# A decoder step on one core: the third token tile's norm emitted behind all output weights

## The chip, the core and the metric

The kernel runs on one core of a Trainium2 chip. The metric is the device time of one execution in microseconds (us). Before the change it is 3105.05 us, the median of three runs (3102.8 to 3105.16).

## What is computed

One step of a hybrid decoder in float32: a gated convolution layer, then a layer of gated sliding-window attention, for 2048 prompt tokens and 32 sample tokens (model width 1024, 2048 convolution channels). The part around the change is the end of the convolution layer:

```python
c = depthwise_conv(v)                       # 31 taps, 2048 channels
c = silu(layernorm(c) * ln_g + ln_b)        # mean and variance over the channels
y = (c * silu(z)) @ w_out                   # 2048 -> 1024
x = x + y
```

`z` is a third of the layer's input product. The attention layer behind it works on `x`.

## The kernel before, in words

Phase A (line 41) makes the input product in tiles of 128 channels by 416 tokens, gates it, runs the convolution and stores its result `c` and the gate `silu(z)` to tensors in HBM, channels on partitions. Every product is made of three TensorE passes: each operand is split into a rounded half (`hi`) and the rest (`lo`), and hi x hi, hi x lo and lo x hi are summed.

Phase B (line 277) does the norm and the output product in token tiles of 128 tokens: sixteen for the prompt, one of 32 for the samples, which comes second to last. Tile 2 is the third. Per tile it has three steps.

- `norm(pos)` (lines 292 to 323) loads the tile of `c` (L297, 1 MB, into one of three buffers by pos % 3) and the tile of the gate (L303, 1 MB, two buffers by pos % 2). VectorE sums over the channels of a partition (L306), TensorE sums over partitions with a matrix of ones (L308), VectorE subtracts the mean (L309); ScalarE squares in two halves through one PSUM buffer (L312), VectorE sums them (L314), TensorE again (L315); ScalarE takes the root (L317), VectorE the reciprocal (L318) and the product (L319); ScalarE does SiLU with gain and bias in 16 pieces (L321); VectorE multiplies by the gate (L322).
- `split(pos, c)` makes the two halves: a cast on ScalarE (L336, `bmh`) and a subtract on VectorE (L337, `bml`). They have two buffers by pos % 2.
- `out(pos, ...)` runs 48 matmuls for each half of the 1024 output columns (L359 to L361), j = 0 and j = 1, adds `x` (L363), sums squares for the next norm (L368) and stores (L371). `rows(pos)` loads the tile of `x` for it (L344).

The output weights are eight blocks of 512 input rows by 512 columns, four for j = 0 and four for j = 1, each loaded in two DMAs of 512 KB. `Weights.ahead` (L234) loads seven of them into buffers that are used later for other weights; the eighth goes through a staging buffer (L257). `Weights.half` casts each 512 KB on ScalarE (L262, `ho`) and subtracts on VectorE or GpSimd (L265, `lo`).

The order of the work is set in three ways. A planner at build time walks the program with estimated durations and fixes for each engine, and for the queue of DMA issues of SyncE (SP), one order; an instruction that is ready goes first if it was emitted earlier, and `high_priority(offset=n)` counts it as emitted n places earlier. On the chip each engine then works strictly in that order. Third, `issue_after(ins)` ties DMA issues behind another issue of the same queue, with no wait for its landing. `d["pace"]` holds the last such issue: each `norm` sets it to its `c` load, each load of `ahead` ties itself behind it and sets it anew, and the staged pair of L257 ties itself behind it without setting it.

Tiles 0 and 1 are normed while phase A's last products run. Then the weights are emitted: j = 0, then `norm(2)`, then j = 1 (lines 387 to 393), and behind them the loop over the tiles, which norms and splits two tiles ahead of the products.

Of the kernel before, what the change touches and what calls it, by code (L numbers as in the profile page):

```python
# [276 lines left out]
def phase_b(tc, d, kc, tail, outer, then):  # L277
# [6 lines left out]
    with ExitStack() as ctx:  # L284
# [7 lines left out]
        def norm(pos):  # L292
            i = order[pos]
            n = 128 if i < 16 else TS
            t0 = i * 128
            c = (pl if pos % 3 == 2 else pe).tile([128, 16, n], F32, tag=f"c{pos % 3}", name=f"bc{i}")
            d["pace"] = nc.sync.dma_start(c, cs[:, :, t0:t0 + n])  # L297
            sz = pe.tile([128, 16, n], F32, tag=f"sz{pos % 2}", name=f"bsz{i}")
            t = t0
            while t < t0 + n:  # L300
                q, o = divmod(t, CW)
                e = min(t0 + n, (q + 1) * CW)
                nc.sync.dma_start(sz[:, :, t - t0:e - t0], sz_d[q].rearrange("a p t -> p a t")[:, :, o:o + e - t])  # L303
                t = e
            s = pe.tile([128, n], F32, tag=f"s{pos % 2}", name=f"bs{i}")
            nc.vector.tensor_reduce(s, c.rearrange("p a t -> p t a"), axis=AX.X, op=ALU.add)  # L306
            ps = pn.tile([128, 2, 128], F32, tag="st", name=f"bst{i}", bufs=2)
            nc.tensor.matmul(ps[:, 0, :n], lhsT=kc.ones, rhs=s, start=True, stop=True)  # L308
            nc.vector.tensor_tensor(c, c, ps[:, 0, :n].unsqueeze(1).to_broadcast([128, 16, n]), op=ALU.subtract)  # L309
            for h in range(2):  # L310
                sq = pn.tile([128, 8, n], F32, tag="sq", name=f"bsq{i}_{h}")
                nc.scalar.activation(sq, c[:, 8 * h:8 * h + 8], AF.Square)  # L312
                v = pe.tile([128, n], F32, tag=f"v{h}{pos % 2}", name=f"bv{i}_{h}")
                nc.vector.tensor_reduce(v, sq.rearrange("p a t -> p t a"), axis=AX.X, op=ALU.add)  # L314
                nc.tensor.matmul(ps[:, 1, :n], lhsT=kc.ones, rhs=v, start=(h == 0), stop=(h == 1))  # L315
            r = pe.tile([128, n], F32, tag=f"r{pos % 2}", name=f"br{i}")
            nc.scalar.activation(r, ps[:, 1, :n], AF.Sqrt, bias=kc.eps)  # L317
            nc.vector.reciprocal(r, r)  # L318
            nc.vector.tensor_tensor(c, c, r.unsqueeze(1).to_broadcast([128, 16, n]), op=ALU.mult)  # L319
            for a in range(16):  # L320
                nc.scalar.activation(c[:, a], c[:, a], AF.Silu, bias=kc.lnb[:, a:a + 1], scale=kc.lng[:, a:a + 1])  # L321
            nc.vector.tensor_tensor(c, c, sz, op=ALU.mult)  # L322
            return c

        def split(pos, c):
            i = order[pos]
            n = 128 if i < 16 else TS
            at = pl if pos % 2 else pm
            if n == TS:
                m2 = at.tile([128, 16, 2 * n], F32R, tag=f"mh{pos % 2}", name=f"bm{i}")  # L330
                mh, ml = m2[:, :, :n], m2[:, :, n:]
            else:
                m2 = None
                mh = at.tile([128, 16, n], F32R, tag=f"mh{pos % 2}", name=f"bmh{i}")
                ml = at.tile([128, 16, n], F32R, tag=f"ml{pos % 2}", name=f"bml{i}")
            nc.scalar.copy(mh, c)  # L336
            nc.vector.tensor_tensor(ml, c, mh.bitcast(F32), op=ALU.subtract)  # L337
            return mh, ml, m2
# [34 lines left out]
        cc, ms = {}, {}  # L373

        def ahead(c):
            if c < 2:
                cc[c] = norm(c)
                if c == 0:
                    ms[0] = split(0, cc[0])
# [6 lines left out]
        pp = pool("b_o", space=PSUM, side="right")  # L386
        ws = [[], []]
        for j, places in enumerate((("w4h", "w4l", "w5h", "w5l"), ("w6h", "w6l", "xh"))):
            if j:
                cc[2] = norm(2)  # L390
            raws = [wts.ahead(wout[j, h], f"o{j}{h}", tag, wx if tag == "xh" else None) for h, tag in enumerate(places)] + [None]
            for h in range(4):
                ws[j].append(wts.half(wout[j, h], f"o{j}{h}", pool=wx if j * h == 3 else None, raws=raws[h]))
        ms[1] = split(1, cc[1])
        for pos in range(15):
            ms[pos + 2] = split(pos + 2, norm(pos + 2) if pos else cc[2])
            if pos == 14:
                norms.close()
                tr = then(pm)
            m, row = ms.pop(pos), rows(pos)  # L400
            for j in range(2):
                out(pos, m, row, j)
# [601 lines left out]
def program(tc, d):  # L1004
# [15 lines left out]
    with tc.tile_pool(name="dram", bufs=1, space=DRAM) as dp, tc.tile_pool(name="k", bufs=1) as pk:  # L1020
        for k, shape in (("c", [16, 128, TT]), ("x1", [TT, 1024]), ("ss", [TT, 1]), ("xts", [128, 8, 2 * TS]),
                         ("xt0", [16, 128, 2, 8, 128]), ("xt1", [4, 128, 16, 4, 128]), ("xt2", [4, 128, 16, 4, 128]), ("u", [3, T, UW]), ("ks", [3, TS, 512]), ("vs", [3, TS, 512]),
                         ("qs", [3, TS, 512]), ("ns", [256, 6]), ("pn", [256, 6]), ("pv", [2, 8, 128, 512]), ("z", [EARLY, 128, 512])):
            d[k] = dp.tile(shape, F32, name="t_" + k)
        d["sz"] = [dp.tile([16, 128, CW], F32, name=f"t_sz{c}") for c in range(NCH)]
        d["copies"] = copies
        kc = Consts(tc, d, pk)
        tail = phase_a(tc, d, kc)
        with ExitStack() as outer:
            pk2 = outer.enter_context(tc.tile_pool(name="k2", bufs=1, reuse_waits="tile"))  # L1030
            for k, w in (("kvnorm", 8), ("bnorm", 8), ("lng", 16), ("lnb", 16)):
                kc.load(pk2, k, [128, w])
            kc.load(pk2, "knorm", [128, 64], d["knorm"].partition_broadcast(128))
            kc.load(pk2, "qnorm", [128, 64], d["qnorm"].partition_broadcast(128))
            kc.load(pk2, "rope_s", [TS, 24])

            def then(pm):

                pool = lambda name, **k: outer.enter_context(tc.tile_pool(name=name, reuse_waits="tile", **k))
                pk3 = pool("k3", bufs=1)  # L1040
                kc.load(pk3, "mask", [128, 3, 128])
                tr = Trunk(tc, d, kc, pk3, pool("c_f", bufs=2), pm, pool("c_pf", bufs=1, space=PSUM))
                tr.banks = {"pj": ("pj", 2), "tr": ("tr", 1)}
                return tr

            wts, tr = phase_b(tc, d, kc, tail, outer, then)
            tc.keep_in_program_order(nc.scalar.preload_act_table_set("natural_log_exp_and_others"))
            phase_d(tc, d, tr, wts, phase_c(tc, d, tr, wts))
        copies(len(pieces))
# [71 lines left out]
```

## Time and profile before

| | |
|---|---|
| median of three runs | 3105.05 us |
| the profiled execution | 3107.33 us |
| its span on the core | 3105.5 us |
| mean granted clock of TensorE | 0.982 |
| TensorE busy | 2998.1 us, 97% |
| VectorE busy | 2181.9 us, 70% |
| ScalarE busy | 1519.0 us, 49% |
| GpSimd busy | 1281.7 us, 41% |

All times in the text are in us from the start of the span. Phase B lies between about 1095 and 1560. In rows, PE is TensorE, PEld its weight loads, DVE VectorE, ACT ScalarE, POOL GpSimd and SPq the issue queue of SyncE; L297 is line 297 of the kernel, and `bml<-bc,bmh` says that `bml` is written from `bc` and `bmh`. A row of a timeline begins with its start and its length, and may be several instructions of one kind (x2). Idle time of an engine before an instruction stands in brackets at its end, with what ended it. "Granted clock" is the share of 2.4 GHz that TensorE was given; 0.5 is its lower level, 1.2 GHz.

### The profile page before, as it was taken

To read this page: it belongs to the slowest core of one execution; us is meant where nothing else is said; L and a number is where in the kernel's file an instruction comes from. 1 tells how busy PE (TensorE), PEld (TensorE's weight loads), DVE (VectorE), ACT (ScalarE), POOL (GpSimd) and SP (SyncE) were. 2 spreads that over 40 slices of the span, in tenths; PEclk is the share of its full clock that TensorE was granted. 3 is DMA by queue.
4 is the path that set the end of the run, shared out by engine and by line. 5 is a ranking of instruction groups with operands and counts; after the bars stand their busy time and mean duration, and the time that the engine had idled before them with its cause. 6 is when DMAs were issued, how large, how long until landed. Compare 5 with 4: busy or idle time off the path is not lost.

```text
span 3105.5 us, 43118 instructions
## 1 busy us (share of the span) xinstructions
PE 2998.1 (97%) x15994; PEld 2542.9 (82%) x15994; DVE 2181.9 (70%) x3698; ACT 1519.0 (49%) x2913; POOL 1281.7 (41%) x809
## 2 busy tenths in 40 slices
PE   6999999999999989999988999999999989999998
PEld 6999999999999977878766777777777767667786
DVE  6599999999999957667555555666666766345355
ACT  6544555555544445566544444554444634444432
POOL 1799889888877603000013222213333041002342
PEclk9999999999999999999989999999999999999999
DMA  6333333434331266444387666778766565653774
GB/s 196 100 106 100 121 106 128 149 116 129 119 128 64 75 190 201 122 132 119 102 211 184 158 170 159 185 221 213 187 159 156 176 205 175 190 178 116 252 254 160
DMA packets 563404, 482.41 MB, mean 155 GB/s; under 512 B 338321, under 2 KB 474129, under 8 KB 555641
## 3 DMA queue, kind: packets, MB, share of 16 engines
q1 hardware_dynamic: 560601, 475.64, 51.9%
q10 hardware_dynamic: 2592, 4.01, 0.4%
q8 instruction: 126, 2.06, 0.3%
q14 instruction: 85, 0.70, 0.1%
HBM read 345.42 MB, written 221.84 MB: 183 GB/s over the span
## 4 chain that ended last, share of the span: by engine, by line
PE 76%; DMA 9%; DVE 7%; ACT 4%; issue 1%; POOL 1%; SPq 1%; ACTq 0%; POOLq 0%; DVEq 0%
PE pv L68 3%; PE pv L70 3%; PE pv L69 3%; PE pg L68 3%; PE pg L70 3%; PE pg L69 3%; PE pz L70 3%; PE pz L68 3%; PE pz L69 3%; PE s L812 3%; PE pjk L536 3%; PE pjk L539 3%; PE pjk L538 3%; PE pt L831 2%; PE ut L840 2%; PE pjq L538 2%
## 5 line engine op out<-in xcount | busy, mean ns | idle before, releaser
L181 POOL TENSOR_TENSOR ca<-ca,tp 128x1024 f32<-128x1024 f32 x288 | 707.3, 2458 | 175.1 <-ACT tp L180 122.6
L196 DVE SCALAR_TENSOR_TENSOR acc<-vb,cws,acc 128x1024 f32<-128x1024 f32 x608 | 754.6, 1281 | 6.5
L180 ACT ACTIVATE tp<-vb,cws 128x1024 f32<-128x1024 f32 x288 | 329.9, 1151 | 288.7 <-POOL ca L181 280.9
L754 POOL COPY ro<-xt 128x512 f32<-128x512 f32 x128 | 149.4, 1175 | 388.5 <-DMA t_xt<-ro 166.7
L633 POOL TENSOR_TENSOR qb<-qb,kc 128x512 f32<-128x512 f32 x96 | 125.6, 1312 | 321.0 <-DMA qb<-t_qs 247.5
L68 PE MATMUL pv<-xh,wh 128*128 128x416 f32 x640 | 225.1, 352 | 3.1 <-DVE vb L109 2.6
L68 PE MATMUL pg<-xh,wh 128*128 128x416 f32 x640 | 226.2, 354 | 1.6 <-ACT xh L151 1.6
L70 PE MATMUL pg<-xh,wl 128*128 128x416 f32 x640 | 227.2, 355 | 0.0
L70 PE MATMUL pz<-xh,wl 128*128 128x416 f32 x640 | 226.5, 354 | 0.0
L70 PE MATMUL pv<-xh,wl 128*128 128x416 f32 x640 | 226.5, 354 | 0.0
L69 PE MATMUL pg<-xl,wh 128*128 128x416 f32 x640 | 225.2, 352 | 0.1
L68 PE MATMUL pz<-xh,wh 128*128 128x416 f32 x640 | 224.6, 351 | 0.0
L69 PE MATMUL pv<-xl,wh 128*128 128x416 f32 x640 | 224.1, 350 | 0.0
L692 POOL MEMSET spq<- 128x24 f32 x8 | 0.9, 118 | 540.2 <-ACT hq L269 371.2
L69 PE MATMUL pz<-xl,wh 128*128 128x416 f32 x640 | 223.6, 349 | 0.0
L823 ACT ACTIVATE sm<-sm,ngm 128x256 f32<-128x256 f32 (+1 forms) x384 | 172.7, 452 | 95.0 <-DVE ngm L820 92.9
L359 PE MATMUL bpo<-ho,bmh 128*128 128x512 f32 x512 | 205.8, 404 | 11.0 <-ACT ho L262 7.8
L360 PE MATMUL bpo<-lo,bmh 128*128 128x512 f32 x512 | 205.1, 401 | 5.3 <-DVE lo L265 3.1
L361 PE MATMUL bpo<-ho,bml 128*128 128x512 f32 x512 | 203.4, 399 | 2.2 <-DVE bml L337 2.1
L834 ACT COPY qp_p<-pt 128x512 f32<-128x512 f32 x150 | 86.3, 585 | 185.3 <-PE pt L831 184.7
L536 PE MATMUL pjk<-hk,xt 128*128 128x512 f32 x384 | 162.4, 423 | 9.8 <-ACT xt L500 9.6
L536 PE MATMUL pjq<-hq,xt 128*128 128x512 f32 x384 | 156.2, 407 | 4.5 <-ACT hnk L547 4.5
(319 smaller groups left out, 7569.0 us busy)
## 6 DMA issues: line engine op xcount, KB each, us to landing
t_xt<-ro SPq DMA_DIRECT2D x128, 256.0 KB
xt<-t_xt SPq DMA_DIRECT2D x32, 1024.0 KB
wr<-in_win SPq DMA_DIRECT2D x48, 512.0 KB
qb<-t_qs SPq DMA_DIRECT2D x96, 256.0 KB
kc<-in_cache SPq DMA_DIRECT2D x72, 256.0 KB
vc<-in_cache SPq DMA_DIRECT2D x72, 256.0 KB
t_c<-ca SPq DMA_DIRECT2D x16, 1040.0 KB
bc<-t_c SPq DMA_DIRECT2D x16, 1024.0 KB
```

What stands on the lines that cost most here:

```text
L68: nc.tensor.matmul(ps, lhsT=hi[:, k], rhs=xh[:, k], start=(k == 0), stop=False)
L69: nc.tensor.matmul(ps, lhsT=hi[:, k], rhs=xl[:, k], start=False, stop=False)
L70: nc.tensor.matmul(ps, lhsT=lo[:, k], rhs=xh[:, k], start=False, stop=(k == 7))
L180: nc.scalar.activation(tp, src, AF.Copy, scale=cws[:, ct, j:j + 1])
L181: nc.gpsimd.tensor_tensor(dst, dst, tp, op=ALU.add)
L196: nc.vector.scalar_tensor_tensor(out if j == KT - 1 else acc[h], vt[:, h * 1024 + j:h * 1024 + j + 1024], cws[:, ct, j:j + 1], out if j == ...
L359: nc.tensor.matmul(po[:n], lhsT=mh[:, a], rhs=hi, start=(a == 0), stop=False)
L360: nc.tensor.matmul(po[:n], lhsT=mh[:, a], rhs=lo, start=False, stop=False)
L361: nc.tensor.matmul(po[:n], lhsT=ml[:, a], rhs=hi, start=False, stop=(a == 15))
L536: first = nc.tensor.matmul(ps[:n], lhsT=xh[:, j], rhs=hi[:, j], start=(k == 0), stop=False)
L538: nc.tensor.matmul(ps[:n], lhsT=xh[:, j], rhs=lo[:, j], start=False, stop=False)
L823: nc.scalar.activation(sm[:, k], sm[:, k], AF.Exp, bias=ngm[:, h:h + 1], scale=0.125, accum_out=u[:, 520 + h:521 + h])
```

## The change

`norm(2)` is emitted after the weights of both column halves, and not between them. Inside `norm`, for tile 2 alone, the issues of its `c` load and of its gate load are tied behind the issue that `d["pace"]` holds at that moment, which is the last load of `ahead` for j = 1. The loads of `ahead` for j = 1 are then tied behind those of j = 0 and no longer behind tile 2's `c` load. Nothing that is computed changes.

```diff
@@ -294,6 +294,10 @@
             n = 128 if i < 16 else TS
             t0 = i * 128
             c = (pl if pos % 3 == 2 else pe).tile([128, 16, n], F32, tag=f"c{pos % 3}", name=f"bc{i}")
+
+            behind = ExitStack()
+            if pos == 2:
+                behind.enter_context(tc.issue_after(d["pace"].ins))
             d["pace"] = nc.sync.dma_start(c, cs[:, :, t0:t0 + n])
             sz = pe.tile([128, 16, n], F32, tag=f"sz{pos % 2}", name=f"bsz{i}")
             t = t0
@@ -302,6 +306,7 @@
                 e = min(t0 + n, (q + 1) * CW)
                 nc.sync.dma_start(sz[:, :, t - t0:e - t0], sz_d[q].rearrange("a p t -> p a t")[:, :, o:o + e - t])
                 t = e
+            behind.close()
             s = pe.tile([128, n], F32, tag=f"s{pos % 2}", name=f"bs{i}")
             nc.vector.tensor_reduce(s, c.rearrange("p a t -> p t a"), axis=AX.X, op=ALU.add)
             ps = pn.tile([128, 2, 128], F32, tag="st", name=f"bst{i}", bufs=2)
@@ -386,11 +391,10 @@
         pp = pool("b_o", space=PSUM, side="right")
         ws = [[], []]
         for j, places in enumerate((("w4h", "w4l", "w5h", "w5l"), ("w6h", "w6l", "xh"))):
-            if j:
-                cc[2] = norm(2)
             raws = [wts.ahead(wout[j, h], f"o{j}{h}", tag, wx if tag == "xh" else None) for h, tag in enumerate(places)] + [None]
             for h in range(4):
                 ws[j].append(wts.half(wout[j, h], f"o{j}{h}", pool=wx if j * h == 3 else None, raws=raws[h]))
+        cc[2] = norm(2)
         ms[1] = split(1, cc[1])
```

## Rows read from the trace of the kernel before

**Rows 1.** Windows: length, busy us (instructions) by engine, granted clock, DMA share, GB/s
```profile
1210.00:1220.00 10.00, 6.17 (x21) 3.83 (x19) 7.44 (x6) 8.64 (x15) 0.00 (x0) 0.79 0.93 256
1220.00:1230.00 10.00, 9.94 (x32) 8.02 (x33) 6.18 (x5) 2.31 (x2) 0.00 (x0) 0.70 1.04 300
...
1400.00:1540.00 140.00, 140.00 (x630) 112.70 (x629) 87.86 (x67) 86.58 (x164) 0.00 (x0) 1.00 0.37 106
```

**Rows 2.** Waits of TensorE, 1200 to 1230: total us, times, longest
```profile
PE bpo L359 <- ACT bmh L336: 3.0, 2, 2.6
PE bpo L361 <- DVE bml L337: 0.9, 1, 0.9
```

**Rows 3.** Chain of waits in order of time, 1150 to 1240: start, length, what
```profile
1164.03 9.71 DMA bc<-t_c
...
1220.03 7.17 DMA bc<-t_c
```

**Rows 4.** Chain of waits in order of time, 1300 to 1600
```profile
1385.96 2.30 DVE bml L337
```

**Rows 5.** Waits of TensorE, 1230 to 1700
```profile
PE bst L315 <- DVE bv L314: 2.6, 1, 2.6
```

**Rows 6.** Timeline of VectorE, 1150 to 1224
```profile
1152.90 3.65 DVE L306 TENSOR_REDUCE bs<-bc 128x128 f32<-128x2048 f32 x1 [6.63 <-DMA bc<-t_c]
...
1173.76 3.79 DVE L306 TENSOR_REDUCE bs<-bc 128x128 f32<-128x2048 f32 x1 [2.74 <-DMA bc<-t_c]
1178.19 4.49 DVE L309 TENSOR_TENSOR bc<-bc,bst 128x2048 f32<-128x2048 f32 x2 [0.64 <-PE bst L308]
1182.60 1.22 DVE L314 TENSOR_REDUCE bv<-bsq 128x128 f32<-128x1024 f32 x1
...
1186.51 0.68 DVE L363 TENSOR_TENSOR bx<-bpo,bx 128x512 f32<-128x512 f32 x1
...
1192.56 3.79 DVE L306 TENSOR_REDUCE bs<-bc 128x128 f32<-128x2048 f32 x1
1196.26 3.33 DVE L319 TENSOR_TENSOR bc<-bc,br 128x2048 f32<-128x2048 f32 x1
...
1205.93 2.29 DVE L322 TENSOR_TENSOR bc<-bc,bsz 128x2048 f32<-128x2048 f32 x1 [1.96 <-ACT bc L321]
...
1217.72 4.48 DVE L337 TENSOR_TENSOR bml<-bc,bmh 128x2048 fp32r<-128x2048 f32 x2
```

**Rows 7.** Timeline of the queue of SyncE, 1139 to 1181
```profile
1139.79 0.36 SPq L303 DMA_DIRECT2D bsz<-t_sz  x1
1146.30 0.36 SPq L297 DMA_DIRECT2D bc<-t_c  x1
1146.78 13.65 SPq L240 DMA_DIRECT2D rawo<-in_wout  x8
...
1164.03 2.07 SPq L297 DMA_DIRECT2D bc<-t_c  x1
1166.19 4.89 SPq L240 DMA_DIRECT2D rawo<-in_wout  x6
1171.13 2.95 SPq L257 DMA_DIRECT2D rawo<-in_wout  x2
```

**Rows 8.** Timeline of ScalarE, 1174 to 1220
```profile
1175.11 1.05 ACT L262 CAST ho<-rawo 128x1024 fp32r<-128x1024 f32 x1 [8.69 <-DMA rawo<-in_wout]
...
1177.69 1.05 ACT L262 CAST ho<-rawo 128x1024 fp32r<-128x1024 f32 x1 [0.31 <-DMA rawo<-in_wout]
...
1184.32 1.02 ACT L312 ACTIVATE bsq<-bc 128x1024 f32<-128x1024 f32 x1
...
1191.29 0.37 ACT L317 ACTIVATE br<-bst,eps 128x128 f32<-128x128 f32 x1
...
1213.20 3.79 ACT L336 CAST bmh<-bc 128x2048 fp32r<-128x2048 f32 x2
```

## The prediction

> **What bounds the kernel now.** TensorE is the busiest engine, so I looked first for the stretches in which it isn't: the table of windows through the phase that the diff touches. It shows full work nearly everywhere, 140.00 of 140 us from 1400 on, and a hole at 1210 to 1230: 6.17 us of work in the first ten, and a granted clock of 0.79 and 0.70 of 2.4 GHz, so part of it at 1.2 GHz [rows 1]. The waits of TensorE name what made the hole: 3.0 us for the rounded half `bmh` and 0.9 for the rest `bml`, the split of a token tile [rows 2]. By the order of the code the products of tiles 0 and 1 come first; they run with no such wait from 1200 on, so this is the split of tile 2, the tile whose norm the change moves.
>
> Next I read the chain of waits in order of time, to see whether that hole sets the end. It does, though not through TensorE. From 1164.03 the chain is tile 2's load (9.71 us), its norm, its split, then at 1220.03 the load of tile 5 into the buffer that tile 2 has left, and so on, load, norm, split, until a last `bml` at 1385.96 [rows 3, 4]. Behind that TensorE has work without a break. So what counts is the end of tile 2's `bml`, the first L337 of two in a row of 4.48 us: 1217.72 + 2.3 = 1220.0 [rows 6]. Later by x, every later step of that chain is later by x, and so is the end. Earlier by x helps while TensorE has slack to give: 3.0 + 0.9 us of waits, 5.1 us of clock (10 times 0.21 + 10 times 0.30) and a wait of 2.6 us further on, 11.6 us in all [rows 1, 2, 5].
>
> The queue of SP comes third, because the change is about its order. Behind the load at 1146.30 it holds eight weight loads (j = 0), the `c` load at 1164.03, six weight loads (j = 1) and the staged pair of L257 [rows 7]. By the code the six stand behind tile 2's `c`, so 1164.03 is tile 2; 1146.30 is tile 3, whose buffer is tile 0's. Tile 3's first reduce runs at 1152.90, tile 2's at 1173.76, both right on their load [rows 6].
>
> **Part 1, the two loads move.** Tile 2's `c` goes behind the six loads, and, if the planner issues the pair first (it has the higher priority and is free to go), behind all eight. What a weight load costs while the queue is full is read from the casts that wait for it: 1175.11 to 1177.69 is two loads, 1.29 us each [rows 8]. Eight are 10.3 us. The bytes ahead of tile 2's landing are then those that had landed by the end of the pair, so its landing moves from 1173.7 to 1184.0: **+10.3**. Nothing that SP waits for in between gives that back: the gate load `sz` that is taken from 1139.79 frees the head of the queue, but behind it stands tile 3's load, which came 6.5 us later by its own wait [rows 7].
>
> The gate load itself now lands behind `c`. No row shows it in this place; at the weights' rate its 1 MB takes 2.6 us, and the whole issue-to-landing of a `c` of the same size under load was 9.71 [rows 3]. So it lands between 1187 and 1194, and is wanted at 1205.93 by L322 [rows 6]: at least 12 us of cover, cost nothing. Behind it in the queue stand the first two `x` loads and tile 4's `c`. The first `x`, wanted at 1186.51 by L363 [rows 6], then lands 1.29 behind the gate load, between 1188 and 1195. If that add keeps its place on VectorE, just behind tile 2's reduce (1184.0 to 1187.8), it holds the engine, and tile 2's sums behind it, for 0 to 7 us. I take nothing, the end at the weights' rate, and keep the 7 for the upper end of the range.
>
> **Part 2, the six weight loads move up** by what tile 2's `c` took, between 2.6 and 9.7 us. TensorE waits for no weight of j = 1 [rows 2], so this is worth nothing by itself; it is worth something by clearing ScalarE and GpSimd before tile 2 arrives.
>
> **Part 3, what stands between tile 2 and its split.** From landing to the end of `bml` are 1220.0 - 1173.7 = 46.3 us, far more than its own steps. The rest is neighbours on in-order engines, and can be read off [rows 6, 8]:
> - To the square root at 1191.29: 17.5 us from the start of the reduce. Own: 3.8, two matmul groups 0.9, the subtract 2.25, two squares of 1.02 and two sums of 1.22 (one PSUM buffer, so in turn), 11.4. Over: 6.1. The second square starts 0.5 after its buffer is free (1182.60 + 1.22), behind weight casts; I put 0.5 down to handovers; the other 5.1 is tile 3's subtract, squares and sums in between.
> - The reduce of tile 4 in front of L319: 3.8, and L319 itself at 3.33 where such an operation takes 2.29: 1.0, beside a GpSimd weight subtract.
> - L322 ends at 1208.2, `bmh` starts at 1213.20 behind tile 3's SiLUs: 5.0.
> - `bmh` is one of two in 3.79, so it ends at 1215.1, and `bml` starts at 1217.72 behind an add and tile 4's subtract: 2.6.
>
> Without the handovers that is 18.0 us of others: 1.5 of weights (0.5 and L319's 1.0), 10.1 of tile 3, 6.4 of tile 4. In the changed order the weights land before tile 2 does: -1.5. Tile 4's load stays behind tile 2's in the queue, so its 6.4 stays. Tile 3 is the open one: its tile has been there since 1152.9, and with tile 2 10.3 us later it can be through its subtract and squares first, -5.1; or the planner keeps them side by side, 0. Its SiLUs would then also run ahead, up to -5.0. Between these ends I take all of the 5.1 and half of the 5.0, 7.6, because a head start of 10.3 us is about as long as the whole of tile 3's share.
>
> **Sum.** +10.3 - 1.5 - 7.6 = +1.2 us on the end of tile 2's split, and on the end. The profiled execution took 3107.33 us (span 3105.5), 2.3 above the median of 3105.05; on the median that is 3106.2, say 3106. What moves in the TensorE hole itself (its 2.6 us of wait, its clock) isn't added: the chain at 1386 takes it back.
>
> One rule of the Trainium skill speaks against the change: DMA: Bandwidth & Descriptors, section Rules for kernel authors, says to issue a transfer early and wait for it late, so that work covers it. By it a load on the chain that is issued later costs its whole delay, the second rival below; the trace bears out the first half, that this load is on the chain.
>
> **The rivals.**
> *Tile 2 runs alone.* With weights and tile 3 through, and tile 4's reduce and subtract set behind, all 18.0 goes: 10.3 - 18.0 = -7.7, 3097.4. For it: the planner prefers tile 2's steps (emitted first), and tile 4's load too is later. Against: its order is fixed at build time from its own estimates, which in the kernel before put tile 3's SiLUs ahead of tile 2's cast. TensorE's slack of 11.6 us is the floor of this case, 3093; a better interleave for the tiles behind could reach a little further, 3091.
> *The load's delay arrives whole.* VectorE keeps its order, the reduce of tile 2 ahead of tile 3's steps, and stands idle from 1173 on until the tile is there at 1184; tile 3 gains no head start. Then only the 1.5 of weights goes: +8.8, 3113.9. It decides as soon as tile 3 gives back less than 2.6 us, for then the end is over 6.2 us later. For it: VectorE already stands idle for such loads (6.63 and 2.74 us here), and tile 3's subtract ran only beside tile 2's at 1178, 22 us after its reduce was through [rows 6]: its head start was wasted before. Against: nothing of the data forces that. With the 7 us of the `x` load it is 3120.9.
> *It does only part of what it says.* Both loads are tied behind the last of the six, not behind the staged pair. If the planner lets `c` go before the pair, it lands 6 x 1.29 = 7.7 later and not 10.3: -1.4 in all, 3103.7. Against: nothing holds the pair back.
>
> **How the numbers follow.** The forecast has 0.36, with a range of its own from 3099 to 3111; tile 2 alone 0.28; the whole delay 0.28; the partial one 0.08. A measurement of this kernel tells about 0.2%, 6.2 us, from no change. Faster by more: 0.28 and 0.02 of the partial case, 0.30. Slower by more: 0.28. Within: 0.42. The range reaches over both rivals, 3091 to 3120.
>
> **What would show it.** In the changed profile tile 2's reduce should start right on its load near 1184, the fourth and later casts of j = 1 should no longer wait, and `bml` of tile 2 should end near 1221. If VectorE has an idle of some 10 us for a `c` load at 1173 to 1184, the second rival holds; if TensorE runs through 1210 to 1225 without a wait and at the full clock, the first. I would be wrong in the root if the end moves and the end of tile 2's `bml` does not, or if the chain up to 1386 becomes one of TensorE.

## The result and the profile after

The changed kernel is slower. Six runs gave a median of 3119.57 us (3111.02 to 3128.29) beside 3104.58 us (3097.68 to 3109.59) for six of the kernel before: a ratio of 1.0051, 95% interval 1.0034 to 1.0068, or 15.8 us (10.6 to 21.1). A second, later set gave 3116.19 us beside 3099.20 us, 1.0041 (1.0026 to 1.0055), 12.7 us. These ratios are not the quotients of the medians, which lie 15.0 and 17.0 us apart. The profiled execution took 3121.14 us, its span 3119.3 us at a mean granted clock of 0.982, as before. The forecast was 3106.

Lines shift by the added code: L301 is now the `c` load, L307 the gate load, L311 the sum over a partition's channels, L313 and L320 the two products with ones, L314 the mean, L317 the squares, L319 their sums, L322 the root, L324 the product, L326 SiLU, L327 the gate, L341 `bmh`, L342 `bml`, L364 to L366 the output products, L368 the add of `x`. In both profiles `bml` of tile 0 ends at the same time (1146.3 before, 1146.0 after), so times of phase B can be set side by side.

The windows of [rows 1], in the changed kernel (same columns):

```profile
1210.00:1220.00 10.00, 0.00 (x0) 0.00 (x0) 9.62 (x8) 9.61 (x24) 0.00 (x0) 0.54 0.25 86
1220.00:1230.00 10.00, 4.24 (x9) 2.82 (x10) 4.38 (x3) 7.56 (x15) 0.00 (x0) 0.50 0.46 128
1400.00:1540.00 140.00, 140.00 (x630) 113.07 (x629) 92.72 (x69) 89.60 (x172) 0.00 (x0) 1.00 0.38 110
```

The hole in TensorE has become a gap: no product at all from 1210 to 1220, 4.24 us of work in the next ten, at the lower clock, and full work again behind it. Its waits from 1195 to 1235 (total us, times, longest), against 3.0 for `bmh` and 0.9 for `bml` in [rows 2]:

```profile
PE bst L320 <- DVE bv L319: 11.9, 1, 11.9
PE bpo L364 <- ACT bmh L341: 4.8, 1, 4.8
PE bpo L366 <- DVE bml L342: 0.3, 1, 0.3
```

TensorE had run all products of tiles 0 and 1 and stood before tile 4's ones product (the 11.9) and then before tile 2's `bmh`. The chain of waits (start, length, what) has the same links as before [rows 3, 4]: tile 2's cast and subtract, tile 5's load into tile 2's buffer, and so on until it leaves VectorE for good:

```profile
1218.66 5.80 ACT bc L326 x15
1224.46 1.80 ACT bmh L341
1226.28 2.30 DVE bml L342
1228.60 5.98 DMA bc<-t_c
...
1381.93 1.14 DVE bv L319
1383.12 0.49 PE bst L320 x2
```

Tile 2's split ends at 1226.28 + 2.29 = 1228.57: 8.6 us later than before. VectorE's timeline, as in [rows 6], shows where:

```profile
1178.25 3.91 DVE L311 TENSOR_REDUCE bs<-bc 128x128 f32<-128x2048 f32 x1 [5.84 <-DMA bc<-t_c]
1183.44 0.69 DVE L368 TENSOR_TENSOR bx<-bpo,bx 128x512 f32<-128x512 f32 x1 [1.28 <-DMA bx<-in_x]
1191.39 4.49 DVE L314 TENSOR_TENSOR bc<-bc,bst 128x2048 f32<-128x2048 f32 x2 [7.25 <-PE bst L313]
...
1198.66 1.22 DVE L319 TENSOR_REDUCE bv<-bsq 128x128 f32<-128x1024 f32 x1
1199.79 3.80 DVE L311 TENSOR_REDUCE bs<-bc 128x128 f32<-128x2048 f32 x1
...
1203.57 1.22 DVE L319 TENSOR_REDUCE bv<-bsq 128x128 f32<-128x1024 f32 x1
...
1208.55 2.29 DVE L324 TENSOR_TENSOR bc<-bc,br 128x2048 f32<-128x2048 f32 x1
...
1217.17 2.29 DVE L327 TENSOR_TENSOR bc<-bc,bsz 128x2048 f32<-128x2048 f32 x1 [0.34 <-ACT bc L326]
...
1226.28 2.29 DVE L342 TENSOR_TENSOR bml<-bc,bmh 128x2048 fp32r<-128x2048 f32 x1 [5.62 <-ACT bmh L341]
```

Tile 2 is reduced at 1178.25, 4.5 us later than before and not 10.3. But the mean is subtracted only at 1191.39, after 7.25 us in which VectorE stands idle for TensorE. Before, 4.4 us lay between these two starts; now 13.1. The timeline of TensorE says why. First the kernel before, then the changed one:

```profile
1177.70 0.68 PE L308 MATMUL bst<-bs,ones 128*128 128x128 f32 x4 [1.57 <-DVE bs L306]
```

```profile
1190.74 0.39 PE L365 MATMUL bpo<-lo,bmh 128*128 128x512 f32 x1
1190.97 0.38 PE L313 MATMUL bst<-bs,ones 128*128 128x128 f32 x2
...
1192.35 0.38 PE L313 MATMUL bst<-bs,ones 128*128 128x128 f32 x2
...
1204.04 0.38 PE L320 MATMUL bst<-bv,ones 128*128 128x128 f32 x2
```

Before, TensorE stands at the ones products of tiles 2 and 3 (x4) and waits for the reduce. After, tile 2's comes with no wait at all, between output products: the reduce is done at 1182.2, and its turn is 8.8 us later. By the program's order this product stood behind 48 output products and now stands behind 122; tile 3's, also ready since long ago, went with it, to 127. The second ones product has its turn at 1204.04, 4.2 us behind its sum (1198.66 + 1.22). Before, it came at 1190.38, 3.8 us behind its sum (1185.37 + 1.22):

```profile
1190.38 0.38 PE L315 MATMUL bst<-bv,ones 128*128 128x128 f32 x2
```

ScalarE, as in [rows 8], and behind it a row of before that was left out there:

```profile
1204.82 1.03 ACT L317 ACTIVATE bsq<-bc 128x1024 f32<-128x1024 f32 x1 [3.88 <-DVE bv L319]
1205.87 1.28 ACT L322 ACT_TABLE_LOAD   x1
1207.16 0.37 ACT L322 ACTIVATE br<-bst,eps 128x128 f32<-128x128 f32 x1
...
1210.88 6.26 ACT L326 ACTIVATE bc<-bc,k_lnb,k_lng 128x128 f32<-128x128 f32 x16 [0.39 <-DVE bc L324]
...
1218.60 5.86 ACT L326 ACTIVATE bc<-bc,k_lnb,k_lng 128x128 f32<-128x128 f32 x15
1224.37 1.88 ACT L341 CAST bmh<-bc 128x2048 fp32r<-128x2048 f32 x1
```

```profile
1190.00 1.28 ACT L317 ACT_TABLE_LOAD   x1
```

Tile 2's root now waits for its place on ScalarE and not for that second product, which was through at 1204.42. It stands behind tile 3's last square (1204.82) and the table load that follows it; that square waited for tile 3's sum (1203.57), and this for tile 4's reduce (1199.79) on VectorE. Before, the two ended side by side: the product at 1190.76, the table load at 1191.28. The cast is still behind 15 SiLUs of tile 3: 1224.37 - (1217.17 + 2.29) = 4.9 us.

The queue of SyncE, as in [rows 7], and one row of before that was left out there:

```profile
1146.49 14.86 SPq L240 DMA_DIRECT2D rawo<-in_wout  x14
1162.16 1.60 SPq L257 DMA_DIRECT2D rawo<-in_wout  x2
1164.77 0.38 SPq L301 DMA_DIRECT2D bc<-t_c  x1
1166.01 8.46 SPq L307 DMA_DIRECT2D bsz<-t_sz  x1
...
1178.09 4.73 SPq L307 DMA_DIRECT2D bsz<-t_sz  x2
```

```profile
1160.53 3.40 SPq L303 DMA_DIRECT2D bsz<-t_sz  x2
```

Tile 2's `c` is indeed behind all sixteen weight loads. But before, tile 3's gate load (1 MB, 1160.53) stood ahead of it, and now that stands behind it (1178.09). So eight loads came in ahead and one load of 1 MB went out. By the packets in the trace of before, eight weight loads (1024 packets of 4096 bytes, 163 ns each) held the sixteen DMA engines for 10.5 us, and that gate load, in rows of 128 and 384 bytes (2048 packets each, 20 and 28 ns), for 6.2 us. The difference, 4.3 us, is about the 4.5 by which tile 2 came later; its load was issued only 0.7 us later.

**How much of the loss this is.** From the starts of TensorE's products: the first 192 output products, up to the first of tile 2, take 59.1 us in the kernel before and 71.8 after; the next 208 take 55.0 and 51.6, since less of the lower clock lies behind the hole (granted clock 0.54 in 1215 to 1225 before, 0.73 in 1226 to 1236 after). Net 9.3 us. Three more profiles with the changed order of phase B (below) have 71.9, 71.9 and 71.8, then 50.8, 51.0 and 52.0; a second one with the old order 60.1 and 54.2. But the first product itself starts earlier, 8.0 to 8.5 us behind tile 0's split in these four and 9.8 and 9.6 in the two with the old order. Counted from that split, the changed order is 7 to 8 us later behind product 400 (130.9 to 131.9 against 123.8 and 123.9), in every profile with it. The rest of phase B is chance as well as order: 289.2 to 294.1 us in the four.

**A second loss, outside the part that the forecast covered.** At the entry of phase C the first query product comes 34.1 us behind the last output product, and 28.8 before. It waits for the first normed key `hnk`, 4.5 us before and 8.7 after:

```profile
PE pjq L536 <- ACT hnk L547: 4.5, 1, 4.5
```

```profile
PE pjq L540 <- ACT hnk L551: 8.7, 1, 8.7
```

ScalarE's timeline there, before and after:

```profile
1586.47 1.33 ACT L269 ACTIVATE hq<-rawq,k_bnorm 128x512 fp32r<-128x512 f32 x2 [8.50 <-DMA rawq<-in_wq]
...
1588.18 0.67 ACT L547 ACTIVATE hnk<-pjk,rstd 128x512 f32<-128x512 f32 x1
```

```profile
1593.68 1.33 ACT L269 ACTIVATE hq<-rawq,k_bnorm 128x512 fp32r<-128x512 f32 x2 [9.27 <-DMA rawq<-in_wq]
...
1599.29 1.33 ACT L269 ACTIVATE hk<-rawk,k_kvnorm 128x512 fp32r<-128x512 f32 x2 [3.81 <-DMA rawk<-in_wkv]
1600.53 0.67 ACT L551 ACTIVATE hnk<-pjk,rstd 128x512 f32<-128x512 f32 x1
```

In the changed kernel `hnk` stands behind two casts of the next key weights and so behind their load. No line of the diff is near it: the planner orders the whole program in one walk.

### The profile page after: what moved, and what is told of

Read it like the earlier page. It is cut to its first block, busy times and chain, and to the rows that moved or that the text cites. A ratio compares the mean times of both kernels' runs of the same rounds, so it can differ in the third digit from the quotient of the medians.

```text
span 3119.3 us, 43115 instructions
## 1 busy us (share of the span) xinstructions
PE 2996.8 (96%) x15994; PEld 2539.5 (81%) x15994; DVE 2180.6 (70%) x3698; ACT 1519.1 (49%) x2913; POOL 1283.7 (41%) x809
## 4 chain that ended last, share of the span: by engine, by line
PE 71%; DVE 11%; DMA 9%; ACT 3%; POOL 3%; issue 2%; SPq 1%; POOLq 0%; DVEq 0%; ACTq 0%
DVE acc L196 4%; PE s L816 3%; PE pg L68 3%; PE pg L70 3%; PE pg L69 3%; PE pv L68 3%; PE pv L70 3%; PE pv L69 3%; PE pjk L540 3%; PE pz L70 3%; PE pz L68 3%; PE pjk L543 3%; PE pz L69 3%; PE pjk L542 2%; PE pjv L540 2%; PE pjq L540 2%
## 5 line engine op out<-in xcount | busy, mean ns | idle before, releaser
L181 POOL TENSOR_TENSOR ca<-ca,tp 128x1024 f32<-128x1024 f32 x288 | 707.1, 2457 | 175.3 <-ACT tp L180 123.9
L364 PE MATMUL bpo<-ho,bmh 128*128 128x512 f32 x512 | 204.7, 401 | 11.1 <-ACT ho L262 6.3
L366 PE MATMUL bpo<-ho,bml 128*128 128x512 f32 x512 | 201.8, 396 | 0.3 <-DVE bml L342 0.3
```

The lines of the kernel that those rows point to most:

```text
L181: nc.gpsimd.tensor_tensor(dst, dst, tp, op=ALU.add)
L364: nc.tensor.matmul(po[:n], lhsT=mh[:, a], rhs=hi, start=(a == 0), stop=False)
L366: nc.tensor.matmul(po[:n], lhsT=ml[:, a], rhs=hi, start=False, stop=(a == 15))
```

## The experiments

Three theories came from the first two profiles. **A**, TensorE's turn: tile 2's ones product was moved back in a fixed order, and the hole follows from that. **B**: the gate load tied behind the weights holds up the queue behind it. **C**: only the later landing counts. Each kernel was timed beside the kernel before; the chips differ by up to 6 us, so ratios count. "Place" is the number of output products ahead of tile 2's first ones product; "split" is the end of tile 2's `bml`, "query" the start of the first query product, both in us behind the end of tile 0's `bml`, from the one profile of each kernel. In the edits, `issue_after` also ties an instruction of TensorE or ScalarE behind another of the same engine in its order.

| kernel | place | split | query | ratio to before (95%) |
|---|---|---|---|---|
| before | 48 | 73.7 | 442.6 | |
| changed | 122 | 82.6 | 455.2 | 1.0051 (1.0034 to 1.0068) |
| changed, second set | 122 | 82.3 | 453.5 | 1.0041 (1.0026 to 1.0055) |
| e1_move_only | 122 | 85.6 | 460.3 | 1.0053 (1.0038 to 1.0068) |
| e2_tie_only | 48 | 66.7 | 435.4 | 0.9986 (0.9977 to 0.9996) |
| e4_turn84 | 84 | 79.8 | 458.4 | 1.0039 (1.0024 to 1.0054) |
| e4c_turn48 | 48 | 69.4 | 432.5 | 0.9982 (0.9970 to 0.9995) |
| e12_turn60 | 60 | 71.6 | 437.5 | 0.9995 (0.9983 to 1.0007) |
| e5b_silu3_after | 122 | 77.5 | 447.1 | 1.0013 (0.9999 to 1.0026) |
| e5_silu3_behind | 48 | 66.2 | 435.5 | 1.0006 (0.9996 to 1.0017) |
| e6_norm_first | 1 | 68.5 | 435.2 | 1.0000 (0.9986 to 1.0013) |
| e9_wq_early | 122 | 82.4 | 452.7 | 1.0046 (1.0028 to 1.0063) |
| e11_hnk_first | 122 | 82.1 | 449.6 | 1.0040 (1.0027 to 1.0053) |
| e10_wq_late | 48 | 74.6 | 442.4 | 0.9996 (0.9984 to 1.0008) |

**The halves of the change.** e1 is the changed kernel without the ties; e2 is the kernel before with them.

```diff
-            if pos == 2:
-                behind.enter_context(tc.issue_after(d["pace"].ins))
```

```diff
+            if j:
+                cc[2] = norm(2)
             raws = [wts.ahead(wout[j, h], f"o{j}{h}", tag, wx if tag == "xh" else None) for h, tag in enumerate(places)] + [None]
...
-        cc[2] = norm(2)
```

> Only the place of emission moves; tile 2's two loads carry no tie. Its c load still stands behind all sixteen weight loads in the queue, its gate load keeps the early place of before (1139.8). Theory A (TensorE's turn): what costs is that the first matrix-of-ones product of tile 2 stands behind 122 output matmuls instead of 48; it does here too, so the end of phase B stays about 7 us later than before and the time 10 to 15 us above before. Rival B (the tied gate load delays what stands behind it in the queue): the time falls back to within 4 us of before.

> Emitted at the old place, with both ties: behind the j = 0 weights, and the j = 1 weights behind them. The first product of ones of tile 2 stands behind 48 matmuls, as before; the gate load, and part of tile 3's, now go between the j = 0 weights and tile 2's c load, so that lands later, by 5 us at a guess from its 1 MB. Theory A: TensorE waits at place 48 for the later tile, some 5 to 7 us instead of 1.6, and tile 2's split ends 3 to 6 us later than before; time 3 to 8 us above before. Rival C (only the landing counts, not the turn): the same 5 us. Rival B: as much above before as the changed kernel, 15 us.

Measured: e1 3122.89 us, e2 3101.65 us, the kernel before 3105.46. The emission alone makes the whole loss, with the gate load free, so B is out. It also moves the place to 122; the ties leave it at 48. The loss is somewhat above the 10 to 15 us expected, and made up otherwise: in e1 the last output product is 17.3 us later than before, and nothing is lost at the entry of phase C. The ties do one thing by themselves: in the nine profiles here of kernels that have them the first output product starts 8.0 to 8.5 us behind tile 0's split, and in e1 and the three others that leave tile 2's gate load at its early place and its norm behind the first weights, 9.6 to 9.8. e2 missed its expectation by its sign. Tile 2 did not land later (its reduce is at 1172.63, 27.9 behind tile 0's split, 27.5 before), because its ties hold it behind the loads of j = 0 only, where it stood anyway; and its cast was free of tile 3's SiLUs. So e2 tells nothing of a later landing.

**TensorE's turn.** The changed kernel with an earlier place: output products from some `a` on are tied behind tile 2's first ones product. The condition below gives 84; with `a >= 0` it is 48 (e4c), with `a >= 4` it is 60 (e12). The edit leaves the loads as in the changed kernel.

```diff
-            nc.tensor.matmul(ps[:, 0, :n], lhsT=kc.ones, rhs=s, start=True, stop=True)
+            first = nc.tensor.matmul(ps[:, 0, :n], lhsT=kc.ones, rhs=s, start=True, stop=True)
+            if pos == 2:
+                d["bst2"] = first
...
+                with ExitStack() as turn:
+                    if pos == 1 or (pos == 0 and j == 1 and a >= 12):
+                        turn.enter_context(tc.issue_after(d["bst2"].ins))
+                    nc.tensor.matmul(po[:n], lhsT=mh[:, a], rhs=hi, start=(a == 0), stop=False)
```

> The changed kernel, with TensorE's order tied so that tile 2's first product of ones comes behind 84 output matmuls instead of 122 (about 1182.6, when its reduce is through). Loads as in the changed kernel. Theory A: tile 2's split ends 3 to 9 us earlier than in the changed kernel, the end of phase B with it; time 3 to 9 us below the changed kernel. Rival C (the landing alone counts): no change against the changed kernel.

> The changed kernel, with tile 2's first product of ones tied ahead of all matmuls behind the first 48, as in the kernel before. Loads as in the changed kernel, so TensorE waits there from about 1174 to 1182 for the reduce, 8 us, and runs at 1.2 GHz for a while. In the fixed order tile 3's first product then comes at 96, behind tile 2's sums. Theory A: tile 2's chain has no tile 3 beside it, its split ends near 1207 to 1212, 16 to 21 us earlier than in the changed kernel; TensorE has lost 8 to 13 us at place 48 but no longer waits at 192; end of phase B 5 to 12 us earlier than in the changed kernel. Rival C: the landing alone counts, and the wait at 48 comes on top: 0 to 8 us later than the changed kernel.

Measured: 3120.19 and 3099.32 us. With the place back at 48 and the load still behind all weights the loss is gone and 5.6 us more; against the changed kernel that is 20 us by the ratios. The planner laid out the rest anew too (tile 3's ones product at 96, the entry of phase C as before the change), so the 20 us belong to the order around the place, not to the place alone. It is more than was expected: the last output product is 17 us earlier than in the changed kernel. C is refuted: the reduce of e4c is at 32.2 behind tile 0's split, as late as in the changed kernel (32.3). TensorE pays for the place by standing at it; its other waits from 1150 to 1300 are those for the first weights, which all these kernels have:

```profile
PE bst L313 <- DVE bs L311: 8.0, 1, 8.0
```

Place 84 missed. The hole shrank (6.9 and 2.0 us of waits), but what stood ahead of the place was late itself:

```profile
PE bpo L369 <- ACT bmh L343: 6.9, 1, 6.9
PE bpo L370 <- POOL lo L265: 4.4, 8, 0.8
...
PE bpo L371 <- DVE bml L344: 2.0, 1, 2.0
```

Eight short waits for GpSimd's weight halves delay the products up to 84, and tile 3's split came 97.1 behind tile 0's, later than in the changed kernel (94.6). Products 193 to 400 took 55.3 us, 4 more than there, which gives the gain back. Its entry to phase C has the second loss as well. So the place acts through all that the planner sets around it.

**Tile 3's SiLUs.** They are tied behind tile 2's cast, on the changed kernel (e5b) and on the kernel before (e5).

```diff
+                if pos == 3:
+                    turn.enter_context(tc.issue_after(d["cast2"].ins))
                 for a in range(16):
                     nc.scalar.activation(c[:, a], c[:, a], AF.Silu, bias=kc.lnb[:, a:a + 1], scale=kc.lng[:, a:a + 1])
...
-            nc.scalar.copy(mh, c)
+            cast = nc.scalar.copy(mh, c)
+            if pos == 2:
+                d["cast2"] = cast
```

> The changed kernel with one tie on ScalarE: tile 3's SiLUs stand behind tile 2's cast bmh (in the changed kernel 15 of them, 4.9 us, stand ahead of it). TensorE's order keeps tile 2's first ones product behind 122 output products. Theory A (the place of that product made the split late, the SiLUs are a second, smaller neighbour): the cast follows the gate product within 2.5 us, the split of tile 2 ends about 5 us earlier than in the changed kernel (its distance from tile 0's split 82.6 to about 77.7, still 4 behind the 73.7 of before), the end of phase B is 3 to 5 us earlier. At the entry of phase C the fourth load of the query weights is back ahead of the loads of ss in SyncE's order: if that is the second loss, another 5.5 us are back there, in all 3108 to 3112. Rival (the SiLUs are the cause, not the turn): phase B ends as before the change or earlier, 7 us under the changed kernel. Rival at phase C (the loss there is chance): the first query product comes 34 us behind the last output product, as in the changed kernel, and not 28.8.

> The kernel before with tile 3's SiLUs behind tile 2's cast on ScalarE, the loads and TensorE's turn (48) as before. Theory A: the cast follows the gate product, the split of tile 2 ends 4 to 5 us earlier (73.7 to about 69 behind tile 0's), TensorE's 2.6 and 0.9 us of waits there go, and the end is 3 to 6 us earlier than before, like the two kernels at place 48 that had no SiLUs ahead of the cast (3099.3 and 3101.7 beside 3105.5). Rival (tile 3's split then comes late and TensorE waits for it): no gain, or up to 5 us slower.

Measured: e5b 3105.74 us beside 3101.38, e5 3103.07 beside 3099.20. In e5b the cast (1217.07) follows the gate product and the SiLUs come behind it, here in ScalarE's timeline:

```profile
1217.07 1.90 ACT L344 CAST bmh<-bc 128x2048 fp32r<-128x2048 f32 x1 [0.84 <-DVE bc L330]
1218.87 6.28 ACT L329 ACTIVATE bc<-bc,k_lnb,k_lng 128x128 f32<-128x128 f32 x16
```

The split is 5.1 us earlier, as worked out, the wait for `bmh` is gone and the one of 11.9 us stays. Some 9 to 12 us of the loss are back (1.0013 against 1.0051 and 1.0041), though the place is still 122. In the profile 4 to 6 us of the gain lie at the entry of phase C, whose order this tie restored too. On the kernel before the same tie makes the split 7.5 us earlier and phase B 5 us shorter in the profile, and the time does not move: a miss.

The four kernels side by side say how far the place reaches. With tile 3's SiLUs ahead of the cast, place 122 puts product 400 7 to 8 us later than place 48, counted from tile 0's split; with them behind it, 10.6 us (126.2 in e5b, 115.6 in e5). The times do not follow alike: 13 to 16 us with the SiLUs ahead, and with them behind 1.0013 and 1.0006, no difference clear of the intervals. So the place is shown to cost TensorE 7 to 11 us of phase B; how much of that reaches the end depends on the rest of the order, in a way that was not found.

**Tile 2 ahead of all weights.** The kernel before with `norm(2)` emitted ahead of the loop over the weights.

```diff
+        cc[2] = norm(2)
         for j, places in enumerate((("w4h", "w4l", "w5h", "w5l"), ("w6h", "w6l", "xh"))):
-            if j:
-                cc[2] = norm(2)
```

> The kernel before with tile 2's norm emitted ahead of both halves of the weights: its c load goes ahead of all output weights and its first ones product stands behind 1 output product and not 48. Theory A (what counts is when the split of tile 2 can end, and TensorE's turn is part of that): the reduce starts some 10 to 15 us earlier, the split ends 10 us earlier or more, no wait for bmh or bml is left at 1205 to 1225; the end moves by what TensorE had to give there, 3.9 us of waits and up to 5 of the slow clock: 3094 to 3101. Rival (the weights pay): the fourteen weight loads come 5 to 9.7 us later, the first output product starts later by as much, and the end is level with before or up to 6 us later, 3105 to 3111.

Measured: 3101.69 beside 3101.38 us. Both were right in part: the reduce is 10.8 us earlier and no wait is left in the hole, but the split is only 5.2 us earlier, and the weights pay at the start, in waits from 1150 on:

```profile
PE bpo L359 <- ACT ho L262: 11.9, 1, 11.9
PE bst L308 <- DVE bs L306: 4.3, 1, 4.3
```

**The entry of phase C.** e9 is the changed kernel with the loads of `ss` (the sums of squares that phase B leaves) behind the fourth load of the query weights in SyncE's queue, as before the change; e10 is the kernel before with that load behind the first of them, as after it; e11 leaves the queue alone and puts `hnk` ahead of the two casts on ScalarE.

```diff
+        first = blocks(0)
         tr.norms()
...
+            with self.tc.issue_after(self.d["staged"].ins):
                 nc.sync.dma_start(self.ss[:, 17 + 4 * r:21 + 4 * r].unsqueeze(2), four[r])
```

```diff
+                        if nm == "q01" and q == 1:
+                            behind.enter_context(self.tc.issue_after(self.d["ss0"].ins))
```

```diff
+                            if nm == "k10":
+                                turn.enter_context(self.tc.issue_after(self.d["hn0"].ins))
                             nc.scalar.activation(h[:, j], raw[:, j], AF.Copy, scale=gk)
```

> The changed kernel with another order in SyncE's queue at the entry of phase C alone: the loads of ss stand behind the fourth staged load of the query weights, as in the kernel before, and not one of them ahead of it. Phase B's order is that of the changed kernel. Theory A2 (5 of the 15 us are lost there: that load stood behind a load that waits for a store to land): the first query product comes 28.8 us behind the last output product and not 34.1, and the end is about 5 us earlier than the changed kernel, 3114 to 3116. Rival (that difference is chance or has another cause): 34 us, and the end as in the changed kernel.

> The kernel before with that one issue swapped the other way: the fourth staged load of the query weights stands behind the first load of ss. Phase B as in the kernel before. Theory A2: the first query product comes about 34 us behind the last output product and not 28.8, and the end is about 5 us later than before, 3109 to 3111. Rival (chance, or the difference is taken back within phase C): no change, 3105.

> The changed kernel once more, for a second profile of it. If the two losses found in its first profile belong to the order and not to chance: the end of tile 2's split again 82 to 83 us behind that of tile 0's (73.7 in the kernel before), a wait of TensorE of about 12 us for tile 4's sums and one of 4 to 5 for bmh, and at the entry of phase C the first query product again 33 to 35 us behind the last output product (28.8 before); 3116 to 3122. If the second is chance, that distance is 28 to 30.

> The changed kernel with one change of ScalarE's order at the entry of phase C: the first normed key (hnk, which frees the bank that the first query product waits for) stands ahead of the two casts of the next key weights, as in the kernel before; in the changed kernel it stands behind them and so behind their load. SyncE's queue is left as it is. Theory A3 (the second loss is this place on ScalarE, not the place of the query weights' load, which e10 acquitted): the first query product comes 28 to 29 us behind the last output product and not 34, phase B is unchanged, and the end is 4 to 6 us earlier than the changed kernel in the same call. Rival (chance, or given back within phase C): the end is that of the changed kernel.

Measured: e9 3117.13 beside 3101.38 us, e10 3101.76 beside the same; the changed kernel again 3116.19 and e11 3110.51 beside 3099.20. The second profile of the changed kernel has both losses again: the split at 82.3, the waits of 11.9 and 4.8 us, and 32.2 us at the entry. The queue is not the cause there: in e10 the load stands behind (1579.44), and `hnk` comes as early as ever:

```profile
1585.16 1.33 ACT L271 ACTIVATE hq<-rawq,k_bnorm 128x512 fp32r<-128x512 f32 x2 [8.59 <-DMA rawq<-in_wq]
...
1586.88 0.67 ACT L550 ACTIVATE hnk<-pjk,rstd 128x512 f32<-128x512 f32 x1
```

ScalarE's order is: `hnk` stands behind the two casts in the changed kernel (34.1 and 32.2 us to the first query product) and in e4_turn84 (35.2), and ahead of them in all other kernels of the table (26.9 to 29.1). e9 is among these, so its edit of the queue does not tell the two apart; e10 and e11 do. e11 moved that place alone, and had 28.3:

```profile
1588.46 1.33 ACT L272 ACTIVATE hq<-rawq,k_bnorm 128x512 fp32r<-128x512 f32 x2 [9.40 <-DMA rawq<-in_wq]
...
1590.17 0.67 ACT L554 ACTIVATE hnk<-pjk,rstd 128x512 f32<-128x512 f32 x1
```

What that is worth at the end is not settled. e9 and e11 have no loss at the entry and stand at 1.0046 and 1.0040, the changed kernel at 1.0051 and 1.0041: a mean gain of 1 us, with intervals of some 5 us each way, though in one set of runs e11's median was 5.7 us below the changed kernel's.

**A version faster than both.**

> The changed kernel with tile 2's first ones product tied behind 60 output products (48 in e4c_turn48, 122 in the changed kernel), to find a version faster than both. Theory A: TensorE's wait of 8.0 us for the reduce at place 48 becomes about 5.3 at place 60 (12 products of 0.227 us run first), the split ends as early as at 48 or up to 2 us later, and the end is 1 to 3 us earlier than e4c_turn48, which stood 6 us under the kernel before: ratio to before 0.997 to 0.9985. Rival (tile 3's sums, which the planner here puts in the middle of tile 2's at place 91, hold tile 2 up): the split 3 us later or more and no gain over place 48.

Measured: 3098.14 beside 3099.20 us; the wait at the place fell from 8.0 to 4.0, but tile 3's sums came between tile 2's, as the rival had it, and the split was 2.2 us later than at place 48. No gain over place 48 came of it. So e4c_turn48, its load behind all the weights, has the lowest ratio: 0.9982 of the kernel before (0.9970 to 0.9995), 5.6 us. The runs do not tell it from e2_tie_only at 0.9986.

## Why the prediction was wrong

It took the slot of tile 2's work on TensorE as given. Step by step:

- **What bounds it: right for these two kernels.** The end of tile 2's split sets the end of TensorE's hole, and both came later together. Where the split is earlier, something else can set it: in e5b tile 4's sums do, the wait of 11.9 us.
- **Part 1: right in its mechanism, mis-sized.** Tile 2 landed 4.5 us later in the profile (4.8 behind tile 0's split), for +10.3. The sixteen weight loads are ahead of it as forecast; the gate load of tile 3, at 1160.53 in a row that I had passed over, had been ahead of it before and no longer is, and its 6.2 us on the DMA engines come off. The gate load of tile 2, which I had put at nothing, gives TensorE the earlier first product, 1.3 us. The `x` load held VectorE for 1.28 us at a moment when it had nothing else to do. Of the rival by the Trainium skill (DMA: Bandwidth & Descriptors, Rules for kernel authors) the sign came true. But with the same late load e4c is faster than before, so by the runs it is not the later landing alone that costs.
- **Part 2: right**, no wait for a weight of j = 1.
- **Part 3: the step that failed.** I listed the neighbours of tile 2's chain on VectorE and ScalarE, and booked TensorE's two product groups at 0.9 us of own work, with no turn to wait for. The first product's turn became 8.8 us. (The second had stood 3.8 us in the queue before, beside tile 3's squares, and was through only 0.5 us before the root; I had named the squares alone.) From the starts in the two profiles: landing +4.5; reduce to mean +8.7; mean to root +2.7; root to the end of the split -7.3; in sum +8.6. The 7.6 that I had taken off for tile 3 did not come where I put it. Tile 3's ones product moved back with tile 2's, to place 127, so its head start was wasted again, and tile 3's squares and SiLUs stayed side by side with tile 2's. What came back is tile 4's reduce ahead of L324 (1199.79: it now stands ahead of tile 3's sum and so of the root, the +2.7), the subtract ahead of `bml`, and the 1.0 of L324 itself: 2.29 us now, with no GpSimd instruction behind 1192.6, against 3.33 [rows 6] with GpSimd at work beside 1.2 us of it, and 4.55 in e2, wholly beside GpSimd. The Trainium skill's GPSIMD Engine Reference, section Specifications, says that GpSimd's SBUF interface is shared with VectorE and contended by VectorE operations with two SBUF inputs, which L324 has; the traces agree, with these three times.
- **Sum.** +1.2 against +8.6 at the split and 8.0 behind product 400. The rival "the load's delay arrives whole" had +8.8, and was right in size by chance: half of it is not the load. Its 3120.9, with 7 us for the `x` load, lies beside the measured time by chance too, since that load held up nothing.
- **What stood outside the sum.** I took the order behind the hole as unchanged. It was planned anew up to the entry of phase C, where the profile shows 3.4 to 5.3 us more. Up to the first query product the two profiles show 12.6 and 10.8 us, for 15.8 and 12.7 measured. Some 7 to 8 of these come with the place, as the profiles at 48 and 60 and those at 122 show. The 3.4 to 5.3 at the entry are seen in the profile; undoing them in e9 and e11 gave 1 us, within the noise. So some 6 to 8 us of the measured loss stay open.

Why the planner gave place 122 is an inference: 74 products at 0.229 us are 17 us, far more than the 4.8 us by which the tile lands later. It fits a planner that holds the load behind eight more weights to be much later than it is. TensorE's order is then strict. In the Trainium skill (Perfetto Trace Analysis, Sequencer Loop) a sequencer reads its instructions one by one and each waits for its semaphores; the trace agrees, with an operand ready at 1182.2 and used at 1190.97 without a wait of TensorE.

## What to carry to other kernels

When a step is moved in a program whose engines work through a fixed order, look at the place of its smallest instruction on the busiest engine: a product of a fraction of a microsecond, placed 74 products later, cost more than the megabytes that were moved: 8.8 us of waiting for its turn, and 4.5 of later landing. In the list of what a chain waits for, the busiest engine's turn belongs beside the neighbours on the others. And compare orders over the whole program, since a planner that walks it once can change a place hundreds of microseconds away.

## What was not expected

- A gain in phase B does not reach the end whole. e2, e5, e6 and e4c have the first query product 7.2, 7.1, 7.4 and 10.2 us earlier than before, behind tile 0's split; the times are 4.3 us less, 1.9 more, level and 5.6 less. Losses came through: e1 17.7 in the profile and 16.5 in time, e4_turn84 15.8 and 12.1. Where the gains go behind that point was not found. One profile says little there: from the first query product to the end the profiled executions took 1510 to 1526 us, and 1510 and 1518 for the changed kernel alone. Its second profiled execution took 3103.44 us, the shortest of its eight.
- A place that makes TensorE wait can be the better one: in e4c it stands 8.0 us for the reduce, and behind that has no wait over 0.6 us until the end of phase B.
